# A hybrid encoder step: memory tiles out of PSUM in 512-column multiplications, the norm's column by transfer, the spreading products between the transposes

## The chip, the cores and the metric

The kernel runs on one NeuronCore of a Trainium2 chip. Its engines work at the same time, each through its own list of instructions in order, and wait for each other with semaphores: TensorE (PE; PEld is its weight load) multiplies matrices into PSUM, ScalarE (ACT) and VectorE (DVE) work elementwise on SBUF and PSUM, GpSimd (POOL) does small elementwise work, and SyncE (SP) issues most of the transfers; ACT and POOL issue some. The transfers of all queues run on 16 DMA engines. The metric is the device time of one execution in microseconds (us), smaller is better.

## The reference, cut to what matters

One layer of an encoder for a prompt of 1024 tokens and a sample of 64, both of width 1024, with 256 memory tokens. What the change touches is the start: the memory tokens are normed, and multiplied with two square weight matrices.

```python
def rms_norm(x, g):
    xf = x.astype(F32)
    y = xf * lax.rsqrt(jnp.mean(xf * xf, axis=-1, keepdims=True) + EPS)
    return (y * g.astype(F32)).astype(x.dtype)

def mem_kv(mem, g, w_k, w_v):
    m = rms_norm(mem, g)
    return ((m @ w_k).reshape(bsz, N_MEM, X_HEADS, X_HEAD_DIM),
            (m @ w_v).reshape(bsz, N_MEM, X_HEADS, X_HEAD_DIM))
...
# in trunk_layer
    h = rms_norm(x, n_pre)
    aq, af, ai, ag, bq, bk, bv, bg, cu, cg = jnp.split(h @ w_in, split_idx, axis=-1)
...
```

Here `g` is `norm_mem`, and `n_pre` is `norm_mix_pre`. Behind it come a gated recurrence, stick-breaking attention, pooling, an output projection and cross-attention to the memory keys and values; none of that is changed.

## The kernel before

All matrix products keep float32 accuracy with two parts: a `hi` part rounded to PE's fast format (ACT's copy) and a `lo` part, the rest (DVE's subtraction). Each product is then three: hi with hi, lo with hi, hi with lo (`mm3`; PE's line 171 is the helper `mm` of every product, 175 the transpose `tr`; 183 is ACT's helper `act`, 187 DVE's `tt`, 191 its `stt`).

The stream of work in the first 100 us:

- **Loads.** `load_tile` brings 11 tiles of 128 rows into `xt` (five buffers): tiles 0 and 1 are memory tokens, then x0 to x8. `prefetch` brings weight blocks of 128 columns into `wraw` (two buffers, 512 KB a block): eight blocks of `w_xk` (called blocks 0 to 7 here), two of `w_in` (8 and 9), then `w_xv` and the rest. All stand in SP's list, in order. The loads of the first five tiles and of blocks 0 and 1 (in halves) are issued at once; a later one waits until its buffer is free. For a weight block that is when the block two before it has been split into `whi` and `wlo`.
- **The memory tiles.** PE transposes a tile in eight pieces of 128 by 128 into two PSUM buffers (`tp`, `mem_T`), so that the model dimension lies on partitions. There the norm's weight is one number per partition and piece: the column `gT`, 128 by 8. `mhi` and `mlo` get the two parts of transposed tile times `gT`. The rows' own factor, 1/rms, is not applied here, but behind the product: it is spread over all partitions as `rbm` (two products `tp<-dg,ones` of `ones` with a diagonal matrix `dg`), and DVE multiplies each block's result with it (`mraw`).
- **The x tiles.** ACT squares a tile (`junk<-xt`, with the sum in `small`), POOL makes 1/rms from the sum (`rstd_of`), DVE multiplies tile, factor and `g1` in place, PE transposes, and ACT and DVE split into `hhi` and `hlo`. `g1` is `norm_mix_pre` spread over the partitions by two row products (`hg<-rows,ones`, one row of ones times 512 columns, line 171) and two ACT copies.
- **Warm-up products** (`warm`, line 311) write to a buffer that nobody reads.

The order of the start is written out by hand: the block under `tc.manual_schedule` in `prep_all` fixes PE's, ACT's and DVE's instructions. What `behind` marks comes after its last ones. All else is ordered by a scheduler with a cost for each operation (`Sched`) and by priorities (`urgent`), at build time; on the chip each engine takes its list as it stands.

Before the change the start makes `gT` from a row, with eight products of 128 by 1 and a copy out of PSUM; memory tile 0 leaves PSUM in eight pairs of one ACT copy (with `gT` as its scale) and one DVE operation; memory tile 1 leaves it in two multiplications of 512 columns into `g1` (free until the row products fill it), which are then split from SBUF. The squares of the memory tiles, the row products for `g1` and the spreading for `rbm` stand behind that.

Of the kernel before, what the change touches and what calls it, by code (L numbers as in the profile page):

```python
# [15 lines left out]
P = 128  # L16
# [17 lines left out]
XT = 5  # L34
# [70 lines left out]
def hybrid_step(  # L105
# [98 lines left out]
    def urgent():  # L204
        return tc.high_priority(offset=URGENT)
# [464 lines left out]
    def main():  # L670
# [24 lines left out]

        xts = {}
# [9 lines left out]
        def prep_all():  # L706
# [3 lines left out]
            gT = pool([P, KT], F32, "gT")  # L710
# [7 lines left out]

            with urgent(), tc.manual_schedule(engines={PE.engine, ACT.engine, DVE.engine}):
                warm(WARM)  # L720
                pg = ps_hg()
                for k in range(KT):
                    mm(pg[:, k:k + 1], gmrow[:, k * P:(k + 1) * P], ones[0:1, 0:1], True, True)
                copy(gT, pg[:, :KT])
                warm(2)
                pts = [mem_T(0, 0), mem_T(0, 1)]
                for half in range(2):
                    for k in range(4):
                        kk = half * 4 + k
                        act(mhi[:, kk, 0:P], pts[half][:, k], AF.Copy, scale=gT[:, kk:kk + 1])  # L730
                        stt(mlo[:, kk, 0:P], pts[half][:, k], gT[:, kk:kk + 1], mhi[:, kk, 0:P].bitcast(F32),
                            ALU.mult, ALU.subtract)
                warm(4)
                pts = [mem_T(1, 0), mem_T(1, 1)]
                warm(12)
                xgs = []
                for half in range(2):
                    ks = slice(half * 4, half * 4 + 4)
                    xg = g1.rearrange("p (k t) -> p k t", t=P)[:, ks]
                    tt(xg, pts[half], gT[:, ks].unsqueeze(2).broadcast_to([P, 4, P]), ALU.mult)  # L740
                    xgs.append(xg)
                wraw, whi, wlo, _ = first[0]
                act(whi[:, 0:4], wraw[:, 0:4], AF.Copy)
                for half in range(2):
                    ks = slice(half * 4, half * 4 + 4)
                    act(mhi[:, ks, P:NMEM], xgs[half], AF.Copy)
                    sub(mlo[:, ks, P:NMEM], xgs[half], mhi[:, ks, P:NMEM].bitcast(F32))
                    if half == 0:
                        act(whi[:, 4:8], wraw[:, 4:8], AF.Copy)
                        sub(wlo[:, 0:4], wraw[:, 0:4], whi[:, 0:4].bitcast(F32))  # L750
                sub(wlo[:, 4:8], wraw[:, 4:8], whi[:, 4:8].bitcast(F32))
                last = [cur["PE"], cur["ACT"], cur["DVE"]]
# [11 lines left out]
            with urgent(), behind():  # L764
# [3 lines left out]
                for i in range(2):  # L768
                    ms = small()
                    act(pool([P, D], BF16, "junk", 1), xts[i], AF.Square, scale=D ** -0.5, accum_out=ms[:, 0:1])  # L770
                    load_tile(i + XT)
                    r = rstd_of(ms[:, 0:1], P)
                    dg = pool([P, P], F32, "dg", 2)
                    tsc(dg, ident, r[:, 0:1], ALU.mult)
                    mm(pr[:, i * P:(i + 1) * P], ones, dg, True, True)
                act(rbm, pr[:, :NMEM], AF.Copy)
            sch.done["rbm"] = max(sch.cur.dep.values())
            with behind():
                for hf in range(2):
                    cs = slice(hf * 512, hf * 512 + 512)  # L780
                    pg = ps_hg()
                    mm(pg, ones[32:33, :], g1row[:, cs], True, True)
                    act(g1[:, cs], pg, AF.Copy)
# [591 lines left out]
```

## Time and profile before

| | |
|---|---|
| time, median of 3 runs | 957.41 us (956.52 to 957.61) |
| the profiled execution's own time | 957.03 us |
| its span | 955.3 us |
| mean granted clock of PE | 0.99 |
| chain that ended last, by engine | PE 86%, DVE 6%, ACT 3%, issue 2%, DMA 2%, POOL 2% |
| moved by DMA | 73.61 MB, 77 GB/s over the span |

The span runs from the first to the last recorded instruction of one profiled execution; the time also holds what lies around it. The chain follows back from the last instruction to what released it, again and again. A busy PE is not a PE at its peak, since products overlap. In the views below "idle before" an instruction is put down to the engine and line that ended it.

### The profile page before, as it was taken

Reading aid. Unit: us, or ns where it says so; the run is one execution under the profiler, and the core shown is the slowest. Engines: PE = TensorE matmul, PEld = TensorE weight load, DVE = VectorE, ACT = ScalarE, POOL = GpSimd, SP = SyncE. Lnnn points to the kernel's source line nnn. Section 1 sums busy time; section 2 is a strip of 40 time slices with the busy share of each in tenths; the row PEclk is TensorE's granted clock in tenths of the full one; section 3 lists DMA queues with packets and bytes.
Section 4 is the critical chain, followed back from the end, with each engine's and each line's share of the span. In section 5 each row is a group of like instructions: output and inputs, shape, how many; then the busy total and the mean of one; then the engine's idle time right before and its main releaser. Section 6 shows DMA issues by size and latency. Waiting matters only on the chain.

```text
span 955.3 us, 18303 instructions
## 1 busy us (share of the span) xinstructions
PE 930.0 (97%) x7466; PEld 868.0 (91%) x7466; DVE 554.8 (58%) x1130; ACT 476.7 (50%) x1007; POOL 110.3 (12%) x194
## 2 busy tenths in 40 slices
PE   7899999999998999999999999999999999999997
PEld 5899999998997998998968877999999999999997
DVE  4776762537737735664386597465575445573343
ACT  4732373666635737893475576343353333342231
POOL 3721440001002001001000000221110000001110
PEclk7999999999999999999999999999999999999999
DMA  6743602011100101011110420322342011232221
GB/s 217 237 135 110 203 29 64 24 45 32 45 24 32 34 35 48 28 38 48 56 59 1 159 66 24 110 89 89 129 137 89 25 64 45 67 110 89 89 93 63
DMA packets 32089, 73.61 MB, mean 77 GB/s; under 512 B 4562, under 2 KB 17026, under 8 KB 32004
## 3 DMA queue, kind: packets, MB, share of 16 engines
q1 hardware_dynamic: 30112, 68.07, 21.7%
q0 software_dynamic: 1888, 4.35, 1.3%
q8 instruction: 59, 0.97, 0.4%
q14 instruction: 26, 0.21, 0.1%
q10 hardware_dynamic: 4, 0.01, 0.0%
HBM read 56.45 MB, written 15.89 MB: 76 GB/s over the span
## 4 chain that ended last, share of the span: by engine, by line
PE 86%; DVE 6%; ACT 3%; issue 2%; DMA 2%; POOL 2%; DVEq 0%; POOLq 0%; ACTq 0%; SPq 0%
PE mm L171 65%; PE hg L171 15%; PE tp L175 5%; DVE sm L587 2%; DVE wlo L187 1%; POOL small L321 1%; DVE sm L187 1%; PE mm L311 1%; ACT whi L183 1%; DMA wraw<-in_w_xk_dram 1%; DMA mkd<-mraw 0%; DMA wraw<-in_w_xq_dram 0%; DVE C L191 0%; DMA vraw<-mvd 0%; DVE hlo L187 0%
## 5 line engine op out<-in xcount | busy, mean ns | idle before, releaser
L171 PE MATMUL mm<-hhi,whi 128*128 128x384 f32 (+2 forms) x1272 | 421.7, 332 | 0.0
L171 PE MATMUL mm<-hlo,whi 128*128 128x384 f32 (+2 forms) x1272 | 413.2, 325 | 0.0
L171 PE MATMUL mm<-hhi,wlo 128*128 128x384 f32 (+2 forms) x1248 | 405.9, 325 | 0.0
L171 PEld LDWEIGHTS mm<-hhi,whi 128*128 128x128 f32 x1272 | 239.3, 188 | 4.5 <-issue 1.1
L171 PEld LDWEIGHTS mm<-hlo,whi 128*128 128x128 f32 x1272 | 239.5, 188 | 1.2 <-issue 1.1
L171 PEld LDWEIGHTS mm<-hhi,wlo 128*128 128x128 f32 x1248 | 234.6, 188 | 0.5 <-issue 0.3
L183 ACT ACTIVATE whi<-wraw 128x1024 fp32r<-128x1024 f32 (+1 forms) x53 | 55.2, 1041 | 86.0 <-PE mm L171 72.3
L187 DVE TENSOR_TENSOR wlo<-wraw,whi 128x1024 fp32r<-128x1024 f32 (+1 forms) x53 | 63.5, 1200 | 44.5 <-ACT whi L183 44.1
L183 ACT ACT_TABLE_LOAD x63 | 80.8, 1283 | 10.3 <-DVE gT L199 6.7
L183 ACT ACTIVATE wraw<-mm 128x384 f32<-128x384 f32 (+3 forms) x51 | 22.9, 450 | 73.1 <-PE mm L171 63.2
L587 DVE TENSOR_TENSOR_SCAN sm<-sm 128x384 f32<-128x384 f32 (+4 forms) x52 | 48.2, 936 | 14.3 <-ACT sm L183 14.3
L183 ACT ACTIVATE sm<-hg 128x384 f32<-128x384 f32 (+4 forms) x104 | 42.3, 484 | 16.2 <-PE hg L171 9.2
L187 DVE TENSOR_TENSOR wraw<-mm,gain 128x384 f32<-128x384 f32 (+1 forms) x48 | 24.3, 509 | 41.9 <-ACT wraw L183 41.7
L1156 POOL TENSOR_TENSOR small<-small 128x1 f32<-128x1 f32 (+1 forms) x18 | 4.2, 235 | 374.4 <-ACT wraw L183 374.4
L171 PE MATMUL mm<-mhi,wlo 128*128 128x256 f32 x128 | 36.1, 291 | 2.5 <-DVE wlo L187 2.5
L321 POOL TENSOR_TENSOR small<-small,mhalf 128x1 f32<-128x1 f32 (+2 forms) x50 | 37.1, 742 | 4.1
L171 PEld LDWEIGHTS hg<-E 128*32 128x32 f32 (+1 forms) x1288 | 24.4, 112 | 13.8 <-issue 6.2
L171 PE MATMUL mm<-mhi,whi 128*128 128x256 f32 x128 | 36.4, 295 | 0.0
L171 PE MATMUL mm<-mlo,whi 128*128 128x256 f32 x128 | 36.2, 293 | 0.0
L404 POOL COPY qf<-q 128x512 f32<-128x512 f32 (+1 forms) x12 | 14.1, 1179 | 180.3 <-PE hg L171 166.6
L187 DVE TENSOR_TENSOR hlo<-tp,hhi 128x512 fp32r<-128x512 f32 (+1 forms) x36 | 22.5, 654 | 20.7 <-ACT hhi L183 20.7
L171 PE MATMUL hg<-E 128*32 128x32 f32 (+1 forms) x1288 | 32.9, 202 | 1.7 <-DVE o_sb L187 1.7
(210 smaller groups left out, 1440.4 us busy)
## 6 DMA issues: line engine op xcount, KB each, us to landing
wraw<-in_w_in_dram SPq DMA_DIRECT2D x28, 512.0 KB, 3.6
xt<-in_x_prompt_dram SPq DMA_DIRECT2D x8, 512.0 KB, 4.5
wraw<-in_w_xv_dram SPq DMA_DIRECT2D x8, 512.0 KB, 3.6
wraw<-in_w_out_dram SPq DMA_DIRECT2D x8, 512.0 KB, 3.6
C<-in_x_prompt_dram SPq DMA_DIRECT2D x8, 512.0 KB, 3.6
x1d<-C SPq DMA_DIRECT2D x8, 512.0 KB, 2.8
wraw<-in_w_xq_dram SPq DMA_DIRECT2D x8, 512.0 KB, 3.5
wraw<-in_w_xo_dram SPq DMA_DIRECT2D x8, 512.0 KB, 3.7
```

The costliest lines, as they stand in the source:

```text
L171: cur['PE'] = PE.matmul(out, lhsT=lhsT, rhs=rhs, start=start, stop=stop, skip_group_check=True)
L175: PE.transpose(out, in_, ident[:n, :n])
L183: cur['ACT'] = ACT.activation(out, in_, func, **kw)
L187: cur['DVE'] = DVE.tensor_tensor(out=out, in0=a, in1=b, op=op)
L311: cur['PE'] = PE.matmul(t[:, :256], lhsT=wz[:, :P], rhs=wz, start=True, stop=True, skip_group_check=True)
L321: POOL.tensor_tensor(out=r[:n, :w], in0=r[:n, :w], in1=mhalf[:n, :w], op=ALU.pow)
L404: POOL.tensor_copy(qf[:, 1, :], qq)
L587: DVE.tensor_tensor_scan(m[:nq, :n][:, ::-1], m[:nq, :n][:, ::-1], m[:nq, :n][:, ::-1], 1.0 if p is None else p[:nq, 0:1], ALU.mult, ALU.min)
L1156: POOL.tensor_tensor(out=ms[:n, 0:1], in0=ms[:n, 0:1], in1=ms[:n, pi:pi + 1], op=ALU.add)
```

## The change

1. `gT` is filled by a transfer from `norm_mem` itself, 1024 single numbers into 128 rows of 8, issued first on ACT's queue; the row of `norm_mix_pre` follows it there. The eight products, the copy and the row are gone.
2. Each half of a memory tile leaves PSUM in one DVE multiplication of 512 columns with `gT` (`scaled`), into a buffer of its own. The buffers are those that the pooling uses later: `s1` and `s2` for tile 0, the two of `u` for tile 1. The two parts are split from SBUF (`high`, `low`). Clearing `u` and the transfer from `state_pool` into it come after that.
3. ACT's first activation is a square of 128 columns of `ones` that nobody reads; ACT's table load stands ahead of it.
4. The squares of the two memory tiles move into the hand-ordered block; the spreading for `rbm` keeps only POOL's part, `dg` and the products behind it.
5. The row products for `g1` stand between the transposes of memory tile 0 and those of tile 1; their copies come behind block 1's split. Warm-up products go from 14 + 2 + 4 + 12 to 14 + 8.
6. The loads of two more x tiles (x3 and x4) are placed behind the spreading, and come out ahead of block 2's load in SP's list.

```diff
@@ prep_all
-            gT = pool([P, KT], F32, "gT")
...
+            def square(i):
+                ms = small()
+                act(pool([P, D], BF16, "junk", 1), xts[i], AF.Square, scale=D ** -0.5, accum_out=ms[:, 0:1])
+                return ms
+
+            def spread(ms, i, pr):
+                r = rstd_of(ms[:, 0:1], P)
+                dg = pool([P, P], F32, "dg", 2)
+                tsc(dg, ident, r[:, 0:1], ALU.mult)
+                mm(pr[:, i * P:(i + 1) * P], ones, dg, True, True)
+
+            def scaled(pt, half, tag):
+                ks = slice(half * 4, half * 4 + 4)
+                xg = pool([P, tot], F32, tag, 2 if tag == "u" else 1)[:, :512].rearrange("p (k t) -> p k t", t=P)
+                tt(xg, pt, gT[:, ks].unsqueeze(2).broadcast_to([P, 4, P]), ALU.mult)
+                return xg
...
+                act(pool([P, D], BF16, "junk", 1)[:, :P], ones, AF.Square)
                 warm(WARM)
-                pg = ps_hg()
-                for k in range(KT):
-                    mm(pg[:, k:k + 1], gmrow[:, k * P:(k + 1) * P], ones[0:1, 0:1], True, True)
-                copy(gT, pg[:, :KT])
-                warm(2)
                 pts = [mem_T(0, 0), mem_T(0, 1)]
-                for half in range(2):
-                    for k in range(4):
-                        kk = half * 4 + k
-                        act(mhi[:, kk, 0:P], pts[half][:, k], AF.Copy, scale=gT[:, kk:kk + 1])
-                        stt(mlo[:, kk, 0:P], pts[half][:, k], gT[:, kk:kk + 1], mhi[:, kk, 0:P].bitcast(F32),
-                            ALU.mult, ALU.subtract)
-                warm(4)
+                pgs = [ps_hg(), ps_hg()]
+                for hf in range(2):
+                    mm(pgs[hf], ones[32:33, :], g1row[:, hf * 512:hf * 512 + 512], True, True)
+                ms0 = square(0)
+                x00 = scaled(pts[0], 0, "s1")
+                high(x00, 0, 0)
+                x01 = scaled(pts[1], 1, "s2")
+                high(x01, 0, 1)
                 pts = [mem_T(1, 0), mem_T(1, 1)]
-                warm(12)
...
+                warm(8)
+                ms1 = square(1)
+                low(x00, 0, 0)
+                x10 = scaled(pts[0], 0, "u")
+                w_high(0)
+                high(x10, 1, 0)
+                x11 = scaled(pts[1], 1, "u")
+                w_high(1)
+                high(x11, 1, 1)
+                low(x10, 1, 0)
+                low(x01, 0, 1)
+                low(x11, 1, 1)
+                w_low(0)
+                w_low(1)
...
+                spread(ms0, 0, pr)
+                spread(ms1, 1, pr)
                 act(rbm, pr[:, :NMEM], AF.Copy)
+                load_tile(XT)
+                load_tile(XT + 1)
+                for hf in range(2):
+                    act(g1[:, hf * 512:hf * 512 + 512], pgs[hf], AF.Copy)
...
-        rows = pool([33, D], F32, "rows")
-        gmrow, g1row = rows[0:1], rows[32:33]
+        g1row = pool([33, D], F32, "rows")[32:33]
+        gT = pool([P, KT], F32, "gT")
         with tc.high_priority(offset=10 * URGENT):
-            ACT.dma_start(gmrow, norm_mem)
+            with nc.allow_non_contiguous_dma("one column per 128 of the norm's weights"):
+                ACT.dma_start(gT, norm_mem.rearrange("o (k p) -> p (o k)", p=P))
             ACT.dma_start(g1row, norm_mix_pre)
```

PE's list from the end of the first 14 warm-up products to the first weight blocks, before (`hg<-ones,rows` is the making of `gT`, `tp<-ident,xt` a memory tile's transposes, `hg<-rows,ones` the row products for `g1`, `tp<-dg,ones` the spreading for `rbm`; "..." stands for warm-up products):

```order
L171 MATMUL hg<-ones,rows 128x1 x8
...
L175 MATMUL tp<-ident,xt 128x128 x8
...
L175 MATMUL tp<-ident,xt 128x128 x8
...
L171 MATMUL hg<-rows,ones 128x512 x2
L171 MATMUL mm<-mhi,whi 128x256 x8
L171 MATMUL mm<-mlo,whi 128x256 x5
L171 MATMUL tp<-dg,ones 128x128
```

And now, in the same place:

```order
L175 MATMUL tp<-ident,xt 128x128 x8
L171 MATMUL hg<-rows,ones 128x512 x2
L175 MATMUL tp<-ident,xt 128x128 x8
...
L171 MATMUL mm<-mhi,whi 128x256 x8
L171 MATMUL mm<-mlo,whi 128x256 x8
L171 MATMUL mm<-mhi,whi 128x256
L171 MATMUL mm<-mhi,wlo 128x256 x4
L171 MATMUL mm<-mlo,whi 128x256
L171 MATMUL mm<-mhi,wlo 128x256 x5
L171 MATMUL mm<-mhi,whi 128x256
L171 MATMUL tp<-dg,ones 128x128 x2
```

The row products went from behind all warm-up products to between the two tiles' transposes; the spreading products went from inside block 0 to behind the first four products of block 1, both together.

ACT's list from the copy of block 1 to that of block 3, before (`whi<-wraw` with 1024 columns are the copies of blocks 1, 2 and 3 in turn; `g_117` is `g1`):

```order
L183 ACTIVATE whi<-wraw 128x1024
L183 ACTIVATE junk,small<-xt 128x1024
L183 ACTIVATE g_117<-hg 128x512
L183 ACTIVATE junk,small<-xt 128x1024
L183 ACTIVATE g_117<-hg 128x512
L183 ACTIVATE junk,small<-xt 128x1024
L183 ACTIVATE whi<-wraw 128x1024
L183 ACTIVATE rbm<-tp 128x256
L183 ACTIVATE junk,small<-xt 128x1024
L183 ACTIVATE hhi_105<-tp 128x4x128 x2
L183 ACTIVATE junk,small<-xt 128x1024
L183 ACTIVATE whi<-wraw 128x1024
```

And now, from the copy of block 1 on:

```order
L183 ACTIVATE whi<-wraw 128x1024
L183 ACTIVATE g_117<-hg 128x512 x2
L183 ACTIVATE junk,small<-xt 128x1024 x2
L183 ACTIVATE rbm<-tp 128x256
L183 ACTIVATE junk,small<-xt 128x1024
L183 ACTIVATE whi<-wraw 128x1024
L183 ACTIVATE hhi_105<-tp 128x4x128 x2
L183 ACTIVATE whi<-wraw 128x1024
```

Block 2's copy now stands behind `rbm` and one more square, and block 3's copy directly behind the copies of x0; the two squares of the memory tiles are gone from here, since they stand earlier.

SP's list of transfers from the first, before (`xt` are tiles, `wraw` with 512 columns are halves of blocks 0 and 1, with 1024 columns blocks 2 and on):

```order
L704 DMA xt<-in_mem_prompt_dram 128x1024 x2
L692 DMA wraw<-in_w_xk_dram 128x512 x2
L704 DMA xt<-in_x_prompt_dram 128x1024
L692 DMA wraw<-in_w_xk_dram 128x512 x2
L704 DMA xt<-in_x_prompt_dram 128x1024 x2
L286 DMA wraw<-in_w_xk_dram 128x1024
L704 DMA xt<-in_x_prompt_dram 128x1024 x2
L286 DMA wraw<-in_w_xk_dram 128x1024 x2
```

And now:

```order
L707 DMA xt<-in_mem_prompt_dram 128x1024 x2
L692 DMA wraw<-in_w_xk_dram 128x512 x2
L707 DMA xt<-in_x_prompt_dram 128x1024
L692 DMA wraw<-in_w_xk_dram 128x512 x2
L707 DMA xt<-in_x_prompt_dram 128x1024 x4
L286 DMA wraw<-in_w_xk_dram 128x1024 x2
```

The loads of x3 and x4 went from between blocks 2 and 3 to ahead of both. From the first product of block 5 on, PE's list is the same as before.

More of the change, by code (lines that the diff above doesn't have):

```diff
@@ L694, in prefetch @@
                     wq[i] = wblock(src)
+        pad = 16
+        so = pad + SEQ + pad
+        tot = so + SMP
         xts = {}
@@ new lines, in high, with low, w_high, w_low @@
+            def high(xg, i, half):
+                act(mhi[:, half * 4:half * 4 + 4, i * P:(i + 1) * P], xg, AF.Copy)
+            def low(xg, i, half):
+                d = (slice(None), slice(half * 4, half * 4 + 4), slice(i * P, (i + 1) * P))
+                sub(mlo[d], xg, mhi[d].bitcast(F32))
+            wraw, whi, wlo, _ = first[0]
+            def w_high(half):
+                ks = slice(half * 4, half * 4 + 4)
+                act(whi[:, ks], wraw[:, ks], AF.Copy)
+            def w_low(half):
+                ks = slice(half * 4, half * 4 + 4)
+                sub(wlo[:, ks], wraw[:, ks], whi[:, ks].bitcast(F32))
@@ L733, in prep_all @@
-                warm(4)
-                pts = [mem_T(1, 0), mem_T(1, 1)]
-                warm(12)
[L736 to L751, printed above, removed]
+                pts = [mem_T(0, 0), mem_T(0, 1)]
@@ L767, in prep_all @@
                 pr = ps_tp()
[L768 to L775, printed above, removed]
+                spread(ms0, 0, pr)
+                spread(ms1, 1, pr)
                 act(rbm, pr[:, :NMEM], AF.Copy)
+                load_tile(XT)
+                load_tile(XT + 1)
+                for hf in range(2):
+                    act(g1[:, hf * 512:hf * 512 + 512], pgs[hf], AF.Copy)
             sch.done["rbm"] = max(sch.cur.dep.values())
[L778 to L783, printed above, removed]
             yield None
@@ L815, in main @@
         sch.spawn(prep_all(), "prep")
-        pad = 16
-        so = pad + SEQ + pad
-        tot = so + SMP
         us = []
```

## The prediction

> **What bounds the kernel now.** I read the page's first part, then the busy time by stretch, the chain that ended last, and the timeline of the first 56 us, which is all that the change touches.
>
> ```profile
> PE 930.0 (97%) x7466; PEld 868.0 (91%) x7466; DVE 554.8 (58%) x1130; ACT 476.7 (50%) x1007; POOL 110.3 (12%) x194
> 70.00:100.00 30.00, 29.96 (x216) 28.33 (x215) 22.63 (x35) 8.11 (x12) 4.28 (x6) 1.00 0.34 108
> ```
>
> TensorE (PE) is busy for 97% of the span; from 70 to 100 us it waits 0.04 us (columns of a stretch: length, then busy time of PE, PEld, DVE, ACT, POOL, granted clock, DMA share, GB/s). So the kernel is bound by PE, and an earlier start of PE's real work is worth its full length if later stages keep up. Real work starts at 21.14 us:
>
> ```profile
> 1.12 3.17 PE mm L311 x14
> 4.29 2.12 PE hg L171 x16
> 6.68 1.28 ACT L183 ACT_TABLE_LOAD   x1 [6.68 <-DVE gT L199]
> 7.98 0.37 ACT L183 ACTIVATE mhi<-tp,gT 128x128 fp32r<-128x128 f32 x1
> 13.35 0.35 DVE L191 SCALAR_TENSOR_TENSOR mlo<-tp,gT,mhi 128x128 fp32r<-128x128 f32 x1 [0.44 <-ACT mhi L183]
> 13.62 0.68 DVE L187 TENSOR_TENSOR g<-tp,gT 128x512 f32<-128x512 f32 x1
> 13.76 1.12 PE tp L175 x4
> 14.34 0.63 ACT L183 ACTIVATE mhi<-g 128x512 fp32r<-128x512 f32 x1 [0.50 <-DVE g L187]
> 14.88 2.56 PE mm L311 x12
> 17.44 3.70 PE hg L171 x4
> 21.14 3.07 PE mm L171 x13
> 29.37 3.44 PE mm L171 x29
> ```
>
> Rows with an engine and an operation are the timeline (start, length), the others the chain. Read down: warm-up products; the norm weights turned into a column (hg); the table load; eight pairs of a ScalarE (ACT) copy and a VectorE (DVE) subtraction, one after another, 7.98 to 13.70, 5.7 us for one memory tile; the second tile's transposes; twelve warm-up products; the row products that spread the other norm's weights (hg, 3.70); then the first weight block. A product takes 3.07/13 = 0.236 us there and 3.44/29 = 0.119 later. The granted clock, eighth number below, is why:
>
> ```profile
> 0.00:10.00 10.00, 6.92 (x44) 5.42 (x44) 1.69 (x19) 2.39 (x4) 3.56 (x14) 1.00 0.82 287
> 10.00:12.00 2.00, 0.75 (x4) 0.42 (x4) 1.13 (x4) 0.99 (x3) 0.00 (x0) 0.89 0.97 389
> 12.00:14.00 2.00, 0.24 (x1) 0.24 (x2) 1.13 (x4) 1.25 (x3) 0.00 (x0) 0.50 0.07 27
> 16.00:18.00 2.00, 2.00 (x8) 1.21 (x7) 2.00 (x5) 2.00 (x3) 0.00 (x0) 0.50 0.00 0
> 24.00:26.00 2.00, 2.00 (x14) 2.00 (x14) 1.03 (x1) 0.68 (x1) 0.79 (x2) 0.69 0.81 320
> ```
>
> It falls to 0.50 after PE idled, stays there under the light products of 14 to 21 us, and comes back in 24:26 (a mean of 0.69 there is 0.50 up to 25.2), 4.1 us after the first weight block began. The DMA share, ninth, is 0.07 and 0.00 in two stretches: the DMA engines stand still too.
>
> **What goes, and what replaces it.** Gone from the path: the column's 2.12 us of products, the table load behind it (now first on ACT, waiting for nothing, under the first load), and the eight pairs. One DVE multiplication by four columns (0.68) and one ACT copy (0.63) take the place of four pairs. PE's idle time falls too, if its inputs come. They hang on one new thing, the column by transfer.
>
> ```profile
> GB/s 0 0 0 0 0 0 0 0 0 0 0 0 218 218 0 137 328 300 382 382 328 300 437 410 410 355 355 410 410 382 382 410 410 273 205 246 277 301 260 221
> DMA to landing us min/median/max: 3.6/4.1/4.7
> q1 hardware_dynamic: 144, 0.52, 30.2%
> q1 hardware_dynamic: 288, 0.02, 6.4%
> out_dram<-u SPq DMA_DIRECT2D x2, 7.5 KB, 1.6
> u<-in_state_pool_dram POOLq DMA_DIRECT2D x2, 7.5 KB, 5.8
> ```
>
> First row: the first 6 us in 40 slices; bytes move from slice 13 on, at 1.8 us. Second row: the two memory tiles land 3.6 and 4.7 us after their issues at 0.8 and 1.2, so at 4.4 and 5.9. Third row: one 512 KB load (a stretch of 5 us from 127): 128 runs of 4 KB and 16 completions are 144 packets, 9 per DMA engine, at 0.302*16*5/144 = 168 ns. Fourth and fifth: two small stores (79.7 to 82.3) of 128 runs of 60 bytes: 288 packets, so a run is a packet, at 0.064*16*2.6/288 = 9.2 ns; they land in 1.6 us on idle queues. The new column is 1024 runs of 4 bytes: 64 packets per engine.
>
> Bounds: served at once, it lands near 3.0 (1.8, 64*9.2 ns = 0.6, and about 0.6 to finish, of the 1.6 that a small store takes). Behind all seven loads, at 13.3: the 389 GB/s of 10:12 ends with them, 3.67 MB, at 12.1. The nearest row is the last one above: two small transfers, issued at 3.1 and 3.7 into the same stretch, took 5.8 us instead of 1.6, yet landed near 9, before the loads ended. So queues share engines, and small runs pay for it. I take one packet in turn with SP's queue: 64 turns let through 7 transfers of 9 packets, five tiles or 2.62 MB. 2.87 MB had moved by 10.0 (287 GB/s), so 9.4; plus 0.6 for the column itself and 0.6 to finish: **10.7**, and 10.9 for the row of the other norm behind it on the same queue.
>
> [...]
>
> **The sum.** PE transposes tile 0 at 4.4 to 5.5 and idles to 10.9, so its clock falls as it did at 12. Row products 3.70 (14.6), second tile's transposes twice some 0.9 (16.4; the four of 13.76 take 1.12 with their end), eight warm-up products at 2.56/12 (18.1). ACT and DVE are ready sooner: half a tile transposed at 15.5, multiplied by 16.2, copied by 16.9. First weight product 18.1 instead of 21.14: **3.0 earlier**. What follows decides whether that lasts:
>
> ```profile
> 18.08 0.33 SPq L286 DMA_DIRECT2D wraw<-in_w_xk_dram  x1
> 21.62 6.37 SPq L286 DMA_DIRECT2D wraw<-in_w_xk_dram  x2
> 19.97 1.05 ACT L183 ACTIVATE junk<-xt 128x1024 bf16<-128x1024 f32 x1
> 20.21 0.27 DVE L238 MEMSET wpl<- 128x256 f32 x1
> 20.91 0.19 ACT L183 ACTIVATION_READ_ACCUMULATOR junk<-xt 128x1 f32 x1
> 21.22 0.35 DVE L245 RECIPROCAL invcnt<-invcnt 128x32 f32<-128x32 f32 x1
> 25.32 1.06 ACT L183 ACTIVATE whi<-wraw 128x1024 fp32r<-128x1024 f32 x1 [2.50 <-PE mm L171]
> 26.41 1.23 DVE L187 TENSOR_TENSOR wlo<-wraw,whi 128x1024 fp32r<-128x1024 f32 x1 [0.16 <-PE mm L171]
> 28.97 1.09 ACT L183 ACTIVATE hhi<-tp 128x512 fp32r<-128x512 f32 x2 [0.91 <-PE tp L175]
> 32.37 1.21 DVE L187 TENSOR_TENSOR wlo<-wraw,whi 128x1024 fp32r<-128x1024 f32 x1
> 34.14 4.79 DMA wraw<-in_w_xk_dram
> 37.30 1.22 DVE L187 TENSOR_TENSOR wlo<-wraw,whi 128x1024 fp32r<-128x1024 f32 x1
> 41.16 1.22 DVE L187 TENSOR_TENSOR wlo<-wraw,whi 128x1024 fp32r<-128x1024 f32 x1
> 53.49 1.22 DVE L187 TENSOR_TENSOR wlo<-wraw,whi 128x1024 fp32r<-128x1024 f32 x1
> ```
>
> The wlo rows end the splits of weight blocks 2, 3, 4, 5 and 8 (blocks from 0; SP loads a block when the split two before it ends). Now ACT takes the row's copies and two squares first, then rbm, which waits for the spreading products behind 28 products: 18 at 0.236 to 22.4, 10 at 0.119 to 23.6, 0.4 for the two. rbm ends 24.4, a square and its read-out (1.05 and 0.19) 25.6, block 2's copy 26.6, its wlo 27.8: **no lead over 27.6**. Block 3 is then helped by the order: its copy comes right behind two of 0.55 (28.7), not behind a further square, and DVE ends its wlo (1.2) at 30.1, not 33.6: 3.5 ahead. Block 4's load starts at 27.8 and lands at 31.5; three squares and one copy put ACT's copy at 33.7; DVE has the late constants before it (20.21 to 21.57, four groups that lay in a gap, with u's memsets some 1.7 us), and ends wlo at 35.5 instead of 38.5: 3.0 ahead. Block 5's load starts at 30.1, not 34.14, and its wlo ends at 37.6, not 42.4: 4.8 ahead. From block 5 on PE has the same rows in both kernels.
>
> POOL's transfer of u now waits for the low halves (17.7, 18.9 by the same walk), ahead of the first square's result at 21.3: covered. On SP two x tiles stand before block 2's load; the later waits for the second tile's transposes (16.4), block 2's load for a split that ends at 20.1: covered. It is 2 us later than 18.08, which the wait for rbm covers.
>
> Leads of 3.0 to 4.8: I take 4.0. The profiled execution took 957.03 (span 955.3 and 1.7 around it); the runs' median is 957.41. 957.0 - 4.0 = **953.0**.
>
> **The rivals.**
> - *The column is there in time* (by 5.1, when the first transposes end). Row products to 7.4 at full clock (half of 3.70, an estimate), transposes to 8.5, warm-up to 9.7: 11.4 earlier. The same walk from there: no wait for rbm, since the spreading products follow block 1's split (13.7) at 14.6; ACT's copies, squares and rbm end at 16.3, block 2's copy at 17.3, and wlo ends at 18.7, 20.9 and 26.4 for blocks 2, 3 and 4 instead of 27.6, 33.6 and 38.5: 9 to 13 sooner, less 1.7 if the clock has fallen (28 products at 0.236 end at 16.3, not 14.6). 11 off: 946 (943.5 to 948.5). For it: the bound of 3.0. Against it: the 5.8 us of u.
> - *In between*, column near 8: 949.5.
> - *The lead is given back.* wlo rows 26.41 to 53.49, seven of them, are 4.5 us apart, while PE needs 24*0.119 + 0.9 = 3.8 per block and tile: loads and splits set the pace there, and block 2 has no lead. Then blocks 3 to 5 only wait elsewhere: 957 (956 to 958).
> - *Slower: the runs of 4 bytes are dear.* Should each cost as much as an average packet of SP (7.6 us/64 = 119 ns, not 9.2), the column lands at 17.6, 6.9 later than taken: 957.0 - 4.0 + 6.9 = 960 (957.5 to 963). It decides from 9.2 + 4.0/64 = 72 ns per run on; no row has runs that short, and the 9.2 ns for 60 bytes speak against it.
>
> **How the numbers follow.** Forecast 0.42 (951 to 955.5), in time 0.28, between 0.10, given back 0.10, slower 0.10. From 944.5 to 958 are nearly all of the forecast and of the two after it, most of "in time", all but 0.01 of "given back", a little of "slower": about 0.85. A difference of 0.2%, 1.9 us, is about the least that a measurement tells from none: faster is 0.37 of the forecast + 0.28 + 0.10 = 0.75; within it 0.05 + 0.09 + 0.02 = 0.16; slower 0.09.
>
> **What would show it.** The DVE row s<-tp,gT starts at about 10.7 (forecast), 5 (in time) or 17 (slower); the first mm<-mhi,whi at 18.1, 9.7 or 25. If it starts as forecast and block 5's wlo ends at 42, the lead was given back. The gap of PE before the row products and the clock in 12 to 20 us show which half of the sum failed. The forecast is wrong if the column lands before 7 or after 14.

## The result and the profile after

The changed kernel takes **946.17 us** (median of 4 runs, 945.58 to 946.59), the kernel before, on the same chip, 957.28 (956.52 to 957.61): a ratio of 0.9889, with a 95% interval of 0.9871 to 0.9908. That is 11.1 us less; the forecast was 953.0, 4.0 less. The sign was right, and the size was less than half of what came. The profiled execution of the changed kernel took 946.23, its span is 944.5.

First the rows of the page and of the busy time by stretch that answer to those of before (columns as there: length, busy time of PE, PEld, DVE, ACT and POOL, granted clock, DMA share, GB/s):

```profile
PE 923.9 (98%) x7440; PEld 863.0 (91%) x7440; DVE 554.9 (59%) x1125; ACT 474.7 (50%) x1002; POOL 106.7 (11%) x194
0.00:10.00 10.00, 8.29 (x43) 5.27 (x44) 4.07 (x17) 6.22 (x11) 4.09 (x16) 1.00 0.83 267
10.00:12.00 2.00, 1.70 (x13) 1.50 (x14) 2.00 (x4) 1.88 (x4) 0.63 (x1) 1.00 1.04 412
12.00:14.00 2.00, 1.80 (x16) 1.59 (x14) 2.00 (x3) 2.00 (x5) 0.00 (x0) 1.00 1.02 406
16.00:18.00 2.00, 1.57 (x15) 1.52 (x14) 1.57 (x3) 1.08 (x3) 1.92 (x4) 1.00 0.91 350
24.00:26.00 2.00, 2.00 (x19) 2.00 (x19) 2.00 (x4) 1.68 (x4) 1.83 (x3) 1.00 0.90 312
70.00:100.00 30.00, 29.00 (x219) 26.62 (x218) 26.81 (x41) 10.26 (x15) 8.52 (x12) 1.00 0.67 194
```

PE has 6 us less to do and 4.7 us less idle time. The granted clock is 1.00 in every row; before, it was 0.50 from 12 to 25 us. The DMA share does not fall to nothing between 12 and 18 us either: the loads of x3 and x4 go out by 9.2 us and those of blocks 2 and 3 from 13.0. The one row that is worse is the last: PE now waits 1.0 us between 70 and 100, where it waited 0.04; what that costs in the end is said where the prediction is answered.

Then the start, from the timeline of the changed kernel (start, length, engine, line, operation, count; in brackets the wait ahead and what ended it):

```profile
0.79 0.47 ACTq L829 DMA_DIRECT2D gT<-in_norm_mem_dram  x1
2.02 1.28 ACT L183 ACT_TABLE_LOAD   x1 [2.02 <-issue]
4.61 1.21 PE L175 MATMUL tp<-ident,xt 128*128 128x128 f32 x8 [0.32 <-DMA xt<-in_mem_prompt_dram]
5.74 1.98 PE L171 MATMUL hg<-rows,ones 1*128 1x512 f32 x4
5.80 1.29 DVE L187 TENSOR_TENSOR s<-tp,gT 128x512 f32<-128x512 f32 x2 [3.95 <-DMA gT<-in_norm_mem_dram]
6.53 1.23 ACT L183 ACTIVATE mhi<-s 128x512 fp32r<-128x512 f32 x2 [0.82 <-DVE s L187]
7.65 1.09 PE L175 MATMUL tp<-ident,xt 128*128 128x128 f32 x8
8.58 1.04 PE L311 MATMUL mm<-ones 128*128 128x256 bf16 x8
9.89 0.74 PE L171 MATMUL mm<-mhi,whi 128*128 128x256 f32 x4 [0.27 <-ACT mhi L183]
18.60 1.22 DVE L187 TENSOR_TENSOR wlo<-wraw,whi 128x1024 fp32r<-128x1024 f32 x1
20.67 1.22 DVE L187 TENSOR_TENSOR wlo<-wraw,whi 128x1024 fp32r<-128x1024 f32 x1
25.91 1.22 DVE L187 TENSOR_TENSOR wlo<-wraw,whi 128x1024 fp32r<-128x1024 f32 x1
28.92 1.22 DVE L187 TENSOR_TENSOR wlo<-wraw,whi 128x1024 fp32r<-128x1024 f32 x1
40.96 1.22 DVE L187 TENSOR_TENSOR wlo<-wraw,whi 128x1024 fp32r<-128x1024 f32 x1
```

The column is there at 5.7, as tile 0's transposes end, and not at 10.7. PE goes from the transposes to the row products without a gap, and those take 1.98 instead of 3.70, as the clock has not fallen. The first weight product is at 9.89, 11.2 us before the old 21.1. The wlo rows, of blocks 2, 3, 4, 5 and 8, stand 7.8, 11.7, 11.4, 12.2 and 12.5 us ahead of those of before, and the span is 10.8 shorter: the lead of the start reaches the end but for 1.7 us.

Last, how the two queues shared the DMA engines (q1 is SP's, q10 is ACT's; packets, MB, share of the 16 engines' time), from 3.3 to 4.5 us:

```profile
q1 hardware_dynamic: 70, 0.22, 53.9%
q10 hardware_dynamic: 985, 0.00, 45.8%
```

In this stretch 985 of the 1042 packets of ACT's queue moved beside 70 of SP's: 14 to 1, not one for one. In its middle, from 3.9 to 4.2 us, the two rows are:

```profile
q10 hardware_dynamic: 421, 0.00, 78.2%
q1 hardware_dynamic: 10, 0.02, 25.7%
```

That is 42 to 1. A run of 4 bytes took 0.458*16*1.2/985 = 8.9 ns.

### The profile page after: what moved, and what is told of

It reads as the page before. It is cut to its first block, busy times and chain, and to the rows that moved or that the text cites. A ratio compares the mean times of both kernels' runs of the same rounds, so it can differ in the third digit from the quotient of the medians.

```text
span 944.5 us, 18234 instructions
## 1 busy us (share of the span) xinstructions
PE 923.9 (98%) x7440; PEld 863.0 (91%) x7440; DVE 554.9 (59%) x1125; ACT 474.7 (50%) x1002; POOL 106.7 (11%) x194
## 3 DMA queue, kind: packets, MB, share of 16 engines
q10 hardware_dynamic: 1042, 0.01, 0.1%
## 4 chain that ended last, share of the span: by engine, by line
PE 83%; DVE 6%; DMA 4%; ACT 2%; issue 2%; POOL 2%; DVEq 0%; POOLq 0%; ACTq 0%
PE mm L171 64%; PE hg L171 15%; PE tp L175 5%; DVE sm L587 3%; DVE sm L187 1%; DVE wlo L187 1%; POOL small L321 1%; DMA wraw<-in_w_xk_dram 1%; DMA xt<-in_x_prompt_dram 1%; DMA mkd<-mraw 1%; DMA gT<-in_norm_mem_dram 1%; DMA wraw<-in_w_xv_dram 1%; DMA mvd<-mtm 0%; ACT whi L183 0%; DVE hlo L187 0%
## 5 line engine op out<-in xcount | busy, mean ns | idle before, releaser
L187 DVE TENSOR_TENSOR wlo<-C,whi 128x1024 fp32r<-128x1024 f32 x16 | 19.6, 1225 | 25.1 <-ACT whi L183 23.6
```

What stands on the lines that cost most here:

```text
L187: cur['DVE'] = DVE.tensor_tensor(out=out, in0=a, in1=b, op=op)
```

## The experiments

All runs in this table were timed beside the kernel before, in three sessions in which its medians were 956.89, 956.88 and 955.61 us; two more kernels, further down, ran once each. First uses and first products are read from each run's trace; the first row of the changed kernel is that of the result, against 957.28.

| kernel | time, us | ratio to before (95%) | first use of the column | first weight product |
|---|---|---|---|---|
| before | 956.9 | 1 | 7.98 | 21.1 |
| changed | 946.17 | 0.9889 (0.9871 to 0.9908) | 5.80 | 9.89 |
| changed, again | 946.15 | 0.9898 (0.9867 to 0.9929) | 5.8 | 10.24 |
| column behind five loads | 952.31 | 0.9964 (0.9947 to 0.9981) | 10.97 | 18.13 |
| the same, with warm-ups | 951.57 | 0.9953 (0.9935 to 0.9972) | 11.8 | 16.95 |
| column behind three loads | 950.78 | 0.9938 (0.9920 to 0.9957) | 8.36 | 15.86 |
| before, with the column by transfer | 954.91 | 0.9978 (0.9965 to 0.9992) | 7.1 | 20.21 |
| changed, tile 0 in eight pairs | 948.51 | 0.9920 (0.9905 to 0.9936) | 5.62 | 13.88 |
| changed, squares and loads behind | 950.61 | 0.9942 (0.9924 to 0.9959) | 5.72 | 10.38 |
| before, with 24 more warm-ups | 955.38 | 0.9992 (0.9979 to 1.0006) | 9.37 | 18.95 |
| 8 runs and a transpose, square moved | 948.65 | 0.9920 (0.9903 to 0.9936) | 5.62 | 13.39 |
| 8 runs and a transpose | 945.74 | 0.9889 (0.9862 to 0.9916) | 5.6 | 10.37 |

### Where the prediction had put the column

```diff
         with tc.high_priority(offset=10 * URGENT):
-                ACT.dma_start(gT, norm_mem.rearrange("o (k p) -> p (o k)", p=P))
-            ACT.dma_start(g1row, norm_mix_pre)
...
         load_tile(2)
         prefetch(1)
+            SP.dma_start(gT, norm_mem.rearrange("o (k p) -> p (o k)", p=P))
+        SP.dma_start(g1row, norm_mix_pre)
```

> The changed kernel, with the column and the row of the other norm issued on SP's queue behind the first five loads (2.62 MB) instead of on ACT's own queue. This puts the column where the prediction had put it. Expected landing: the five loads are in by about 9.4 to 10, and 1.2 more makes 10.5 to 11.2. Theory A (only the landing was wrong, the rest of the prediction holds): PE idles 5.5 to about 10.7, the clock falls to 0.50, the first weight product starts at 17.5 to 18.6, and the kernel takes 952 to 954. Theory B (the start passes on one for one, as 9.89 against 21.07 gave 11): 946.2 + 8.2 = 954.4 with the first product at 18.1; A and B differ by little and are not told apart by this run. Rival C (the gain comes from the new order of the squares, the spreading products and the loads of x3 and x4, and the column's time matters little): 946 to 948.

The timeline and the stretches of that run:

```profile
10.97 1.29 DVE L187 TENSOR_TENSOR s<-tp,gT 128x512 f32<-128x512 f32 x2 [9.12 <-DMA gT<-in_norm_mem_dram]
11.10 3.77 PE L171 MATMUL hg<-rows,ones 1*128 1x512 f32 x4 [4.57 <-DMA rows<-in_norm_mix_pre_dram]
18.13 2.06 PE L171 MATMUL mm<-mhi,whi 128*128 128x256 f32 x8
26.02 1.16 DVE L187 TENSOR_TENSOR wlo<-wraw,whi 128x1024 fp32r<-128x1024 f32 x1
28.03 1.22 DVE L187 TENSOR_TENSOR wlo<-wraw,whi 128x1024 fp32r<-128x1024 f32 x1
33.24 1.22 DVE L187 TENSOR_TENSOR wlo<-wraw,whi 128x1024 fp32r<-128x1024 f32 x1
36.62 1.22 DVE L187 TENSOR_TENSOR wlo<-wraw,whi 128x1024 fp32r<-128x1024 f32 x1
8.00:10.00 2.00, 0.00 (x0) 0.00 (x0) 0.00 (x0) 0.00 (x0) 0.00 (x0) 0.99 1.08 308
10.00:12.00 2.00, 0.90 (x1) 0.49 (x2) 1.03 (x2) 0.30 (x1) 0.00 (x0) 0.50 0.96 340
```

The column is there at 10.97 (forecast 10.7), PE idles, the clock falls to 0.50 at 10 us, the row products take 3.77 (3.70), the first weight product comes at 18.13 (18.1), and the kernel takes 952.3 (953.0). PE's and DVE's lists of instructions are those of the changed kernel, so one thing alone was wrong in the sum: when the column lands. The rival by which the column's time matters little falls: 952.3 is not 946. A delay passed on one for one (954.4) is not told apart from it by this run; the next one does that.

### The column a little late, and the clock

The same edit with the two transfers behind three loads (after `prefetch(0)`):

> As the run with the column behind five loads, but behind the first three (1.57 MB): the column should land at 7 to 8. If the end follows the landing one for one, 946.2 + 7.5 - 5.7 = 948 while the clock stays near 1.0; if PE's idle stretch of about 2 us is enough to bring the clock down, the first weight product is late by 1.8 and some 3 more, and the time is 951. If the column's time matters little: 946.

```profile
8.92 3.77 PE L171 MATMUL hg<-rows,ones 1*128 1x512 f32 x4 [2.83 <-DMA rows<-in_norm_mix_pre_dram]
12.63 1.97 PE L175 MATMUL tp<-ident,xt 128*128 128x128 f32 x8
14.39 1.71 PE L311 MATMUL mm<-ones 128*128 128x256 bf16 x8
15.86 1.19 PE L171 MATMUL mm<-mhi,whi 128*128 128x256 f32 x8
```

The column is used at 8.36 (expected 7 to 8), 2.6 us later than in the changed kernel, and the first weight product comes 6.0 later. The difference is the clock: PE idles 2.83 us ahead of the row products, the granted clock is 0.50 from 8.9 to 15.8 us, and in that time these take 3.77 instead of 1.98, the transposes 1.97 instead of 1.09, the warm-ups 1.71 instead of 1.04, together 3.3 us more. The time, 950.8, is the second branch of the expectation (951). So this late landing is paid for twice, and between 5.7 and 8.4 us the price is not one for one.

Warm-ups in that idle stretch should take the second payment away:

```diff
                 pts = [mem_T(0, 0), mem_T(0, 1)]
+                warm(36)
                 pgs = [ps_hg(), ps_hg()]
```

> The kernel with the column behind five loads, and 36 warm-up products in PE's idle stretch between tile 0's transposes and the row products (they compute nothing). It takes the clock out of that run: column again at 10.5 to 11.2; with the clock at 1.0 the row products take 1.98 instead of 3.77, the second tile's transposes 1.1 instead of 1.97, and the first weight product comes at 14.5 to 15 instead of 18.13. Then some 3.4 of the 8.2 us between the late and the changed kernel's first products are the clock, and the time is 949 to 950.5. If the fall of the clock costs nothing behind the first product: 952 again.

It does so only in part: the column came at 11.8 in this run's trace, the 36 products were through at 9.5, PE waited 2.5 us for the row, and the clock fell at 14. The row products kept full speed (1.98), the transposes and warm-ups did not (1.72 and 1.91). 951.6 beside 952.3, with overlapping intervals: this run does not tell the shares apart.

### The transfer by itself

```diff
                     act(mhi[:, ks, P:NMEM], xgs[half], AF.Copy)
+                    if half == 0:
+                            ACT.dma_start(gX, norm_mem.rearrange("o (k p) -> p (o k)", p=P))
...
+                copy(gY, gX)
                 last = [cur["PE"], cur["ACT"], cur["DVE"]]
```

> The kernel before, with a second transfer of the same column (1024 runs of 4 bytes) issued from ACT's queue at about 15 us, where the DMA engines stand still, into a tile that one small DVE copy at the end of the start reads and nothing else. It measures the transfer alone. If SP's loads took turns with it in the changed kernel, it lands much sooner here than the 4.9 us of there: about 1.6 to 2.5. If the transfer mostly took its own fixed time there, and the loads cost it little: 4 to 5 us here as well.

The DMA rows of that run, from 15 to 18.5 and from 17 to 18 us:

```profile
gX<-in_norm_mem_dram ACTq DMA_DIRECT2D x1, 4.0 KB, 2.4
q10 hardware_dynamic: 1010, 0.00, 55.4%
```

The one execution of this kernel took 956.91 us. Alone the column lands 2.4 us after its issue; beside SP's loads it took 4.9, and 5.0 and 4.5 in two other traces that issue it first on ACT's queue (the kernel before with the column by transfer, and the changed kernel again). That is the first branch of the expectation, but not for the reason given there, since the loads slow the runs themselves little: 980 of them move in 0.6 us alone (17.1 to 17.7), 939 in 0.9 us beside the loads (3.6 to 4.5). Most of the 2.5 us lies ahead of them (they set in 1.4 us after the issue here, 2.8 there) and behind them (0.4 and 1.2 us to the landing). Why they start and end later beside loads was not tried.

With four more such transfers ahead of it:

```diff
+                for c in range(4):
+                    ACT.dma_start(gX[:, c * KT:(c + 1) * KT], norm_mix_pre.rearrange("o (k p) -> p (o k)", p=P))
                 ACT.dma_start(gT, norm_mem.rearrange("o (k p) -> p (o k)", p=P))
```

> The changed kernel with four more transfers of the same shape (1024 runs of 4 bytes each, of the other norm's weights, into a tile that nothing reads) ahead of the column on ACT's queue: 320 runs per DMA engine instead of 64. Theory of bursts (the engine takes a queue's short runs many at a time at 9.2 ns each, beside SP's loads): the column lands at 5.7 + 4 * 0.6 = 8.1, up to 9 if each transfer's issue (0.47) and SP's loads come between. Theory of one packet in turn with SP's queue, as the prediction had it: 320 turns are more than the 63 packets per engine of all seven loads, so it lands with their end, 13 or later. In bursts, the kernel takes about 949 in one look; in turns 956 or more.

Timeline, then the queues from 8 to 10 us:

```profile
0.80 5.49 ACTq L831 DMA_DIRECT2D gX<-in_norm_mix_pre_dram  x4
6.32 0.61 ACTq L832 DMA_DIRECT2D gT<-in_norm_mem_dram  x1
q10 hardware_dynamic: 2068, 0.01, 57.9%
q1 hardware_dynamic: 118, 0.28, 49.6%
```

Both expectations missed the landing, 11.8 us: ACT needed 5.49 us to issue four such transfers, 1.37 each instead of 0.47, so the column itself was issued at 6.32 and landed 5.5 later. On the sharing the rows are plain. With work waiting on both queues, ACT's moved 2068 runs beside SP's 118, 17.5 to 1, at 9.0 ns each; over these 2 us the two shared the engines' time about by halves. They did not do so evenly: the rate is 328 GB/s at 8.0 us and 9 to 10 from 8.75 to 9.0, where hardly anything but short runs can have moved. The loads paid: the rate of 8 to 10 us is 147 GB/s, 308 in the run with the late column. The one execution took 953.8 us.

With each of these runs as a packet, as the profile counts them, 14 and 17.5 to 1 speak against one packet in turn with SP's queue; in the shorter stretch from 3.9 to 4.2 us the ratio was 42 to 1. What sets the ratio is not settled by these runs.

### The parts of the change, one at a time

The kernel before, with the column by transfer and nothing else (its eight products, the copy and `warm(2)` left out):

> The kernel before with one thing changed: the norm column comes by the strided transfer on ACT's queue instead of eight products, a copy and two warm-ups. The eight pairs, the row products behind the warm-ups, the squares and the loads stay as before. The column lands at 5.7 again; the table load (1.28) still stands behind it, so the pairs start at 7.0 instead of 7.98: 956 (955 to 957), no difference that can be measured. Rival: the transferred column is itself the source of the gain: 950 or less.

954.9: 2.0 us less than before, just below the expected range and far from 946, so the rival falls. The pairs start at 7.1 instead of 7.98.

The changed kernel with tile 0 in eight pairs again:

```diff
-                x00 = scaled(pts[0], 0, "s1")
-                high(x00, 0, 0)
-                x01 = scaled(pts[1], 1, "s2")
-                high(x01, 0, 1)
+                for half in range(2):
+                    for k in range(4):
+                        kk = half * 4 + k
+                        act(mhi[:, kk, 0:P], pts[half][:, k], AF.Copy, scale=gT[:, kk:kk + 1])
+                        stt(mlo[:, kk, 0:P], pts[half][:, k], gT[:, kk:kk + 1], mhi[:, kk, 0:P].bitcast(F32),
...
```

> The changed kernel with memory tile 0 taken out of PSUM in eight pairs of an ACT copy and a DVE subtraction, as before; all else as changed. A pair took 0.71 (5.7/8), so eight end at 5.8 + 5.7 = 11.5, and the second tile's multiplication, behind them on DVE, starts at 11.6 instead of 8.34: first weight product at about 13.2 instead of 9.89. In the runs with a late column 2.3 us of the first product were 1.5 at the end, so + 2.2 to 3.3: 948.4 to 949.5 if the clock stays at 1.0. PE then idles some 2.4 us between tile 0's last transposes and tile 1's second half; it fell after idle stretches of 2.8 and 3.5 us. If it falls here too, row products are already done, but warm-ups and the first products run at half: 950 to 952. Rival (the gain comes from the column and the row products alone): 946 to 947.

948.5: 2.3 us more than the changed kernel. The first product came at 13.88, later than expected, as the clock did fall; the end lost less than the start, so the sum of the second branch was too dear. But it did not fall for the reason expected:

```profile
5.56 1.98 PE L171 MATMUL hg<-rows,ones 1*128 1x512 f32 x4
8.79 1.11 PE L175 MATMUL tp<-ident,xt 128*128 128x128 f32 x4 [1.25 <-DVE mlo L191]
0.00:10.00 10.00, 7.26 (x30) 4.18 (x30) 2.68 (x17) 4.98 (x11) 3.31 (x14) 0.88 0.82 272
```

A mean clock of 0.88 over 10 us, with 0.50 from 10 to 14, is 1.00 up to 7.6 and 0.50 from there, if it fell once; 0.90 from 14 to 16 puts its return at 14.4. PE had been busy without a gap from 4.57 to 7.54, with transposes and the row products, and its two idle stretches of 1.25 and 1.50 us came after the fall. So the 2.3 us hold the price of a low clock that PE's waits for the pairs did not bring about; what the pairs alone cost is not told apart.

The changed kernel with the squares and the two loads where they were:

```diff
-                ms0 = square(0)
...
-                ms1 = square(1)
...
-                spread(ms0, 0, pr)
-                spread(ms1, 1, pr)
+                for i in range(2):
+                    ms = square(i)
+                    load_tile(i + XT)
+                    spread(ms, i, pr)
```

> The changed kernel with the two squares of the memory tiles and the loads of x3 and x4 back where they stood before, behind block 1's split; the column, the 512-column multiplications and the early row products stay. If this move carries part of the gain: two squares (2.5 us of ACT) stand ahead of rbm and block 2's copy again, wlo of block 2 starts at 21 instead of 18.60, and the time is 947.5 to 949. If it carries none, since PE has 3.8 us of other work per block: 946 to 947.

Here the measurement is beyond both: 950.6, 4.4 us more than the changed kernel, though the first weight product is late by 0.5 us only. DVE's first normalisation of an x tile and the stretches tell why:

```profile
10.38 0.74 PE L171 MATMUL mm<-mhi,whi 128*128 128x256 f32 x4
19.63 1.28 DVE L191 SCALAR_TENSOR_TENSOR xt<-xt,small,g 128x1024 f32<-128x1024 f32 x1 [1.38 <-POOL small L321]
20.00:22.00 2.00, 0.94 (x9) 0.96 (x10) 1.25 (x2) 0.27 (x1) 1.84 (x5) 1.00 0.64 215
22.00:24.00 2.00, 0.37 (x4) 0.16 (x2) 1.78 (x2) 1.92 (x5) 1.38 (x4) 0.82 0.47 95
24.00:26.00 2.00, 1.31 (x6) 1.31 (x7) 2.00 (x4) 2.00 (x4) 1.75 (x4) 0.50 0.97 334
26.00:30.00 4.00, 4.00 (x21) 4.00 (x21) 3.36 (x3) 1.67 (x4) 2.87 (x3) 0.50 0.43 142
```

Tile x0 is normalised at 19.63 (15.07 in the changed kernel) and block 2's wlo at 23.42 (18.60). PE, through with block 1, has little to do from 20 to 24 us, and the clock falls at 23.3 and is back at 30. Here the early first product was worth its length only with this work early too. The run moves the squares and the two loads back together, so the share of each is not known.

The kernel before, with 24 more warm-ups in its idle stretch:

> The kernel before, with 24 more warm-up products behind the first tile's transposes, which compute nothing, and nothing else changed: PE is busy where it idled and the clock fell. If the low clock is a cost of its own in the kernel before: clock 1.0 up to 26 us, row products 1.98 instead of 3.70, twelve warm-ups 1.6 instead of 2.56, first weight product at about 18 instead of 21.07, and 0.119 instead of 0.236 for the 28 products behind it, in all 5 to 6.5 earlier at block 2: 951 to 953. If the loads and splits behind set the pace anyway, so that an early block 1 only waits: 956 to 957.

955.4, no difference: the forecast gain missed.

```profile
17.05 1.98 PE L171 MATMUL hg<-rows,ones 1*128 1x512 f32 x4
18.00:20.00 2.00, 2.00 (x10) 1.23 (x9) 2.00 (x3) 2.00 (x5) 0.52 (x1) 0.89 0.05 6
```

The row products ran at full speed and the first weight product came at 18.95 instead of 21.1, but the clock fell at 19.6 all the same, 0.5 us behind the row products, though PE had been busy without a gap since 15.64; it was 0.50 from 20 to 22 us. Block 2's wlo, behind its load and the squares, started at 27.12 instead of 26.41. In this profiled execution PE was also slower at the start (the eight pairs began at 9.37 instead of 7.98), which the twelve timed runs need not share. A busy PE alone buys nothing that can be measured there.

### A version that needs no short runs

```diff
-                ACT.dma_start(gT, norm_mem.rearrange("o (k p) -> p (o k)", p=P))
+            ACT.dma_start(g8, norm_mem.rearrange("o (k p) -> (o k) p", p=P))
...
                 warm(WARM)
+                pg = ps_hg()
+                tr(pg[:, :KT], g8, KT)
+                copy(gT, pg[:, :KT])
                 pts = [mem_T(0, 0), mem_T(0, 1)]
```

First together with the second square moved behind the copies of tile 1:

> A version that may beat both: the norm's weights come as 8 runs of 512 bytes into an 8 x 128 tile, one PE transpose and one small DVE copy make the column of it (instead of 1024 runs of 4 bytes), and the second square stands behind the copies of tile 1 on ACT. If the landing is set by the transfer's fixed part and SP's loads ahead of it, and short runs cost only 9.2 ns: the row lands at 4.2 to 4.8, the column is there at 5.0 to 5.3, DVE's first multiplication starts at 5.3 instead of 5.80, and the first weight product at about 9.0 instead of 9.89: 945 to 946, too little to measure. If the 1024 short runs slowed the loads beside them, tile 1 lands earlier too (before 5.2 us after its issue).

948.7, slower than the changed kernel. In that trace PE ran at half rate up to 13 us (the eight warm-ups at 11.82 took 1.92 us, 1.04 in the changed kernel), and x0 was normalised at 20.62. The 1024 short runs do hold up the loads beside them: memory tile 1 landed 5.6 us after its issue in the changed kernel and 4.7 before the change, and from 3.3 to 4.5 us SP's queue moved 0.22 MB there and 0.47 before. To tell the square from the slow start, the square went back:

> The changed kernel with one thing changed: the norm's weights come as 8 runs of 512 bytes, and one PE transpose and one small DVE copy make the column. The second square stands where the changed kernel has it, which the earlier run of this kind had moved as well. If the moved square was what made that run 948.65: 945.5 to 946.5 here, with DVE's first multiplication at 5.2 to 5.7. If it was the start (PE's products at half rate up to 13 us in that profile, as the transpose stands ahead of tile 0's): 948 to 949 again.

945.7 (0.9889), beside 946.15 (0.9898) for the changed kernel in the same session: no difference. So the moved square is the likely cost: the runs of the two, 947.85 to 949.59 and 943.83 to 946.98, do not overlap. It is not quite shown, since the two were timed in different sessions, and in the profiles PE's slow start alone explains the first product (13.39 against 10.37):

```profile
6.36 3.77 PE L171 MATMUL hg<-rows,ones 1*128 1x512 f32 x4
```

That is the row of the run with the moved square; with the square back the row products start at 6.36 too and take 1.98. The column is there at 4.7 in the second run, 1.0 us sooner than by short runs, and it helps nothing: DVE's first multiplication then waits for tile 0's transposes, at 5.61.

> The changed kernel itself, word for word, timed with the others on the same chip. Expected: 946.2 again (945.5 to 947.5). If the point at which PE's products go from 0.23 to 0.13 us at the start (4.2 to over 6 us in the profiles so far) varies from execution to execution, its runs spread by 1 us or more, and the profiled first weight product is elsewhere than at 9.89.

946.15 again, in runs from 943.84 to 949.93, so a single execution of this kernel is good to some 3 us only. The profiled first weight product is at 10.24 instead of 9.89; tile 0's transposes alone took 0.4 us longer (1.60 for 1.21, the last section).

## Why the prediction was wrong in size

**The step that failed** is the landing: "I take one packet in turn with SP's queue: 64 turns let through 7 transfers of 9 packets". It put the column at 10.7; it landed at 5.7. No run shows such turns. From 3.3 to 4.5 us the engines served 14 of the runs of 4 bytes for one of 2 or 4 KB, and 985 of the 1042 packets of ACT's queue were through in these 1.2 us. The nearest row that the prediction leaned on, u's 5.8 us into the same stretch, was the better measure and was misread as a sign of turns: counted from the column's issue at 0.79 it gives 6.6, while the turns gave 10.7. The two counts of packets that it read, 144 and 288, tell that the profile counts each run as a packet; neither tells how packets of two queues are interleaved.

**All that hung on it.** PE's idle time from 5.5 to 10.9, the fall of the clock, row products at 3.70 and products at 0.236 were derived from that landing and did not happen. With the landing put back where the prediction had it, they do, and the time is 952.3 for 953.0. One term was too long there: the clock came back 2 us after the first weight product and not 4.1, so about 9 products and not 18 ran at 0.23 us each.

**The walk behind it** was right to about 1 us. With the late column, wlo of blocks 2, 3, 4 and 5 ends at 27.18, 29.25, 34.46 and 37.84; the prediction had 27.8, 30.1, 35.5 and 37.6. For the column in time it had a first product at 9.7 and wlo ends of 18.7, 20.9 and 26.4; measured 9.89, and 19.82, 21.89 and 27.13. Its time for that case, 946, is what was measured, in part by luck: the 11 us in it were picked from leads of 9 to 13, the wlo ends came 0.7 to 1.1 us later than the walk had them, and the lead that reached the end is 10.8 only because of the clock, as told below. The mistake was the chance: 0.28 for the case that came, 0.42 for the one that did not.

**The price of a run.** 9.2 ns, taken from stores of 60 byte runs, holds for 4 byte runs (8.8 to 9.0). The rival that made them dear falls.

**The lead given back.** It was a fear for 0.10; 1.7 us of 12.5 were given back, and hardly any of it to loads and splits. PE's new wait of 1.0 us between 70 and 100 us is nearly made up, as PE before the change waited 0.76 between 100 and 115: the wlo rows stand 12.3 us ahead at 72 us (71.89 and 84.17) and still 12.1 at 138 (137.56 and 149.70). The lead goes from 12.1 to 10.5 between 278 and 288 us, where the granted clock of the changed kernel's profile is 0.50 for 6.8 us; before the change it was so for 3.4 us at the same work, and in the second profile of the changed kernel a mean clock of 0.998 over 944.2 us leaves some 4 us at 0.50 in the whole span (an estimate). So this loss differs between executions of one kernel, and what brings the clock down there was not tried.

**What the parts are worth.** Undone one at a time: tile 0's pairs 2.3 us, squares and loads 4.4, a column as late as forecast 6.1; the column alone, done to the kernel before, 2.0. The runs are of different sessions; by their ratios to the kernel before, against the changed kernel's two ratios, the first three are 2.1 to 3.0, 4.2 to 5.1 and 6.3 to 7.2. They do not add up to 11.1 and need not: in each of the three, undone, the clock falls and is paid for too, for the late column and the squares in an idle stretch of PE, for the pairs ahead of one. The early table load and the new place of the row products were not undone alone, so their shares are not known. The prediction did credit the order of the squares, but as a help to block 3; that it also keeps PE from idling at 20 to 24 us was not in it.

## What to carry to other kernels

The 1024 short runs on a queue of their own were not stuck behind the long runs of SP's (they landed 4.9 us after their issue, where turns gave 9.9), though they held those up (memory tile 1 landed 0.9 us later than before): look for the duration of such a transfer in any trace where two queues were busy, and take that before a model of turns. Where PE's start hangs on one small input, price its lateness with the clock as well: 2.6 us of a late column were 6.0 us of the first weight product and 4.6 of the time. And when a stage is made to start earlier, move the work that feeds the next stage (here two squares and two loads) along with it, or the lead is spent in a new gap: left behind, they cost 4.4 us here.

## What the runs showed of the hardware

PE's products at the start ran at half rate for a time that changed from execution to execution, and the granted clock did not show it. Tile 0's eight transposes, the same instructions after the same 14 warm-ups, from the timelines of the changed kernel, the same kernel again, and the run with the late column:

```profile
4.61 1.21 PE L175 MATMUL tp<-ident,xt 128*128 128x128 f32 x8 [0.32 <-DMA xt<-in_mem_prompt_dram]
4.69 1.60 PE L175 MATMUL tp<-ident,xt 128*128 128x128 f32 x8 [0.41 <-DMA xt<-in_mem_prompt_dram]
4.59 1.94 PE L175 MATMUL tp<-ident,xt 128*128 128x128 f32 x8 [0.31 <-DMA xt<-in_mem_prompt_dram]
```

They take 1.04 to 1.97 us in all the runs, and the granted clock reads 1.00 there in each. In the run with five columns the row products took 3.78 at 12.6 us, half speed, in stretches whose granted clock reads 1.00 too, and so did those of the transfer by itself at 18.75. So a clock of 1.00 in these views does not prove full speed; the length of a known product does. What sets the moment at which full speed begins is not shown. The price at the first weight product was some 0.4 us between two executions of the changed kernel (9.89 and 10.24), but 3.0 in the run with the moved square (13.39 and 10.37), where the half rate lasted to 13 us. What makes it last so long is not shown.

In two runs the clock fell behind the row products though PE was busy: with tile 0 in pairs at 7.6 us, with 24 more warm-ups at 19.6, each within 0.6 us of their end. They use 1 of the 128 rows that the other products use (1*128 and 128*128 in the views); that this is the reason is not shown, as the changed kernel has them at 5.74 to 7.72 and keeps its clock.

A transfer of 1024 short runs also cost its issuer: one alone took 0.47 us of ACT's queue, but 1.37 each when four followed one another. SP's issuing came later too: its load of x1 goes out at 6.09 in the changed kernel, at 4.37 before and at 4.43 with 8 runs, and with five columns its third load goes out at 5.30 instead of 1.71.
